# Two rates for the attention filler, E2's pieces split early, and priority for the factor of each norm

## The chip, the cores and the metric

The kernel runs on one core of one Trainium2 chip. The metric is the device time of one execution in microseconds (us); the time of a kernel is the median over several runs. All products are fp32: every operand is split into a high and a low part of the type fp32r, and three matmuls (high by high, high by low, low by high) make one product. Most of the work of ACT and DVE is to make these parts: ACT casts the high part, DVE subtracts it from the source to get the low part.

## The reference, cut to what matters

```python
D_MODEL, SEQ, DEPTH = 1024, 512, 2      # one layer of each kind
MLA_HEADS, NOPE_DIM, ROPE_DIM, V_DIM = 8, 128, 64, 128
B_HEADS, B_HEAD_DIM = 16, 64
...
# layer 0: x = x + post_norm(mla_mixer(pre_norm(x)));   x = x + post_norm(swiglu(pre_norm(x)))
# between: k_band, v_band = shared_kv(x)
# layer 1: x = x + post_norm(chunked_mixer(pre_norm(x), k_band, v_band));  x = x + post_norm(swiglu(pre_norm(x)))
def rms_norm(x, g):
    return x * lax.rsqrt(jnp.mean(x * x, axis=-1, keepdims=True) + EPS) * g
def swiglu(h, w_gate, w_up, w_down):
    return (jax.nn.silu(h @ w_gate) * (h @ w_up)) @ w_down
# a mixer: q, k, v by projections; p = softmax(q k^T + bias or mask); (p v) @ w_o
```

## The kernel before

The 512 rows of x are held transposed, features on the partitions, as eight tiles of 128x512. The stages follow one another: projections, the first attention (8 heads), its out product with `w_o`, a norm, the feed-forward part with its down product, a norm, the shared keys and values, the second attention (16 heads), its out product, a norm, the feed-forward part, and a last norm that writes the output.

A framework places the instructions on the engines by a priority that follows the order in which the code records them; each engine then runs its list in order, and waits there for whatever an instruction needs. `first(n)` records what stands inside it with a priority n earlier.

*Attention.* `attention()` runs over slots, one for each head and query tile of 128 rows. A slot makes the scores (tiles `sc`, from `qh`, `ql`, `kh`, `kl`) and their softmax: a DVE operation that adds the bias and takes the row's extreme (`mn`), then an ACT exponential. Two slots later the probabilities are transposed and split (`turn`, tiles `pth` and `ptl`), and later all of a head is multiplied with its values (`pv`). Between these steps `weave(upto)` takes matmuls from the `Filler`, a generator of units: the projections of the coming heads, then the first three of seven products of the out product. `upto` is the number of units that should be done by this slot; it grows at one rate from `first` to `units`. If head h begins and its projection is not done, `start_a(h)` forces the rest of it at once (`fill.until`).

*Out and down products.* They use seven block products in place of eight: A11, A22, A12, E1, E2, E3 and E6 are products of sums and differences of blocks. For the out product the order is A11, A22, A12, E2, E3, E1, E6. `Rows` makes the left operands, `os` tiles of 128x512 that hold two 128x256 pieces each; a product in its list `now` has each piece split (tiles `ph`, `pl`) as soon as it exists, any other has whole tiles split shortly before use (`ahead`).

```python
self.w, self.rows, self.banks = w, Rows(KT, w.order, lambda n: U(name="os"),
                                        (Seven.A22, Seven.A12, Seven.A11)), {}
```

`seven()` runs the remaining four products in groups of weight tiles; `post.during(j, group)` is called after each group, `post.product(j, ...)` after each product.

*The norm behind a product.* `After.put` (L1146 to L1150) copies a first product's bank into a tile `y`, adds a second bank to it (DVE), and takes its square with a sum per row (ACT, tiles `sq` and `ss`). `rstd` and `power` make the factor: two small DVE operations (`ssv`), then a power on POOL (`r`, L1182). `scale` (L1190) multiplies the `y` tiles with it on ACT. `turn` (L1209) transposes them on TensorE (`yt`), adds the result to `x` (L1212), and splits the new x for the feed-forward part (`xh`, `xl`, L150 and L151). The rows are done in two halves of 256. The second half's transposes stand within the first matmuls of the feed-forward part: `half(0)` gives 18 of its products, each three matmuls of 128x256 on `xh` and `xl`, then `post.turn(1)` follows. Before, `fetch` loads the eight tiles of x (SP's queue) before the remaining four products begin.

Weights are loaded by DMA into `raw` tiles (five buffers) and split into `whi` and `wlo` (three buffers each). `U` tiles, 40 buffers, serve for x, pieces, `y` and much else.

Of the kernel before, what the change touches and what calls it, by code (L numbers as in the profile page):

```python
# [21 lines left out]
H_A, NOPE, ROPE, VD = 8, 128, 64, 128  # L22
QL, KVL = 384, 256
H_B, HD = 16, 64
# [44 lines left out]
def trunk(ctx: ExitStack, tc: tile.TileContext, a, out):  # L69
# [57 lines left out]
    G_APRE, G_APOST, G_FPRE, G_FPOST = (0, 1), (2, 3), (4, 5), (6, 7)  # L127
# [25 lines left out]
    class Pair:  # L153
# [4 lines left out]
        def __init__(self, src):  # L158
            self.src, self.raw = src, {}
# [29 lines left out]
    class Seven:  # L189
# [23 lines left out]
        def fetch(self, to, i, q):  # L213
            n, src, tag = self.width(i), self.src[q, i], self.homes[to][i]
            if tag in ("u", "h"):
                parts = []
                for c in range(0, n, S):
                    t = U(name="wd") if tag == "u" else wide[0].tile([P, S], F32, tag="h", name=name_("wd"), bufs=2 * NF - 4)
                    nc.sync.dma_start(t, src[:, c:c + S])
                    parts.append(t)  # L220
            else:
                t = (wp if tag == "raw" else wide[0]).tile([P, 1024], F32, tag=tag, name=name_("raw"),
                                                           bufs=5 if tag == "raw" else 2)
                nc.sync.dma_start(t[:, :n], src[:, :n])
                parts = [t[:, :n]]
            self.at[to, i] = parts
# [129 lines left out]
    def halves_of(make):  # L356

        return lambda: [(make(), make()) for _ in range(2)]
# [29 lines left out]
    def cut(t, c):  # L388
        return t[0][:, c], t[1][:, c]
# [125 lines left out]
            q_ = slice(qt * P, (qt + 1) * P)  # L515
            split(self.pt[0][:, :qt + 1, q_], self.pt[1][:, :qt + 1, q_], tv)

    def attention(n_heads, start, fill, first, units, after):


        slots = n_heads * NQT
        heads, done, late = {}, [0], []
        rate = (units - first) / slots

        def weave(upto):
            n = 0
            while (n < 4 if fill.scored else done[0] < upto) and fill.step():
                done[0] += 1
                n += 1

        for i in range(slots + 3):
            h, qt = divmod(i, NQT)
            if h < n_heads:
                if qt == 0:
                    heads[h] = start(h)
                    if h == 0:
                        weave(first)
                heads[h].scores(qt)
                fill.scored = i == slots - 1
            weave(first + rate * (i + 0.5))  # L540
            if late and not after:
                late.pop()()
            if i >= 6 and i % NQT == 2:
                t = heads.pop((i - 6) // NQT)
                late.append(t.pv(*t.pt))
                fill.weighed = not heads
            if 2 <= i < slots + 2:
                t, qt = divmod(i - 2, NQT)
                heads[t].turn(qt)
            if late and i % NQT == 3:  # L550
                late.pop()()
            weave(first + rate * (i + 1))
        if late:
            late.pop()()

# [132 lines left out]
    class Out:  # L688
# [2 lines left out]

        def __init__(self, w):
            self.w, self.rows, self.banks = w, Rows(KT, w.order, lambda n: U(name="os"),
                                                    (Seven.A22, Seven.A12, Seven.A11)), {}

        def first(self):
            late = []
# [74 lines left out]
    x = []  # L772
# [19 lines left out]
    xs, sx = [], Sum()  # L792
    b1 = [bank() for _ in range(3)]
    for k in range(KT):
        h, l = U(F32R, "xh"), U(F32R, "xl")
# [66 lines left out]
    for j in range(2):  # L862
        V.tensor_tensor(ckv[j], ckv[j], rkv, op=OP.mult)
        h, l = U(F32R, "ckh"), U(F32R, "ckl")
# [9 lines left out]
    for j in range(3):  # L874
        h, l = U(F32R, "cqh"), U(F32R, "cql")
# [134 lines left out]
        return Head(qk, lambda n: mask[:, S - n:], lambda qt: nsq[:, qt:qt + 1], pv, sums)  # L1010

    fill = Filler(fill_a())
    attention(H_A, start_a, fill, 13, 8 + 5 * 7 + 6 + 6, False)
    fill.drain()
    st.close()

# [1 line left out]
    def ffn(i, x_src, oo):  # L1018
        hp = tc.tile_pool(name=f"ffn{i}", bufs=1, reuse_waits="tile")
        st = ExitStack()  # L1020
        hp = st.enter_context(hp)

        wide[0] = hp

        def H(dt=F32, name="h"):
            return hp.tile([P, S], dt, tag="h", name=name_(name), bufs=2 * NF - 4)

        feed.room["h"] = halves_of(lambda: H(F32R, "wh"))
        post = After(G_APOST[i], None, H)
        post.x = fetch(x_src)  # L1030
        sx = post.split = Split(post.x, G_FPRE[i], H)
        oo.rest(post)
        x, xs = post.x, sx.xs
        banks = [bank() for _ in range(4)]
        ws = []

        def half(h):
            for c in range(4):
                if not h:
                    ws.append(feed.next(1024))  # L1040
                for k in (2 * c, 2 * c + 1):
                    for j in range(4):
                        mm3(banks[j][:, HALF[h]], ws[c]((k % 2) * S + j * P, P), cut(xs[k], HALF[h]),
                            k == 0, k == KT - 1)
                        yield

        rest = half(0)
        some(rest, 18)
        post.turn(1)
        run(rest)  # L1050
        sx.squares(0)
        run(half(1))
        sx.squares(1)
        for k in range(KT):
            nc.sync.dma_start(a["mid"][:, k], x[k])
        tb = []
        more = blocks_of(x, G_FPRE[i], H, tb)
# [12 lines left out]
        hid = Rows(NF, range(7), lambda n: (U if n >= NF - 2 else H)(name="hd"))  # L1070


        for f in range(N_WHOLE):
            if f < 3:
                b = banks[2 * f:2 * f + 2]
                if f == 2:
                    run(rest)
            else:
                b = [bank(), bank()]
                run(proj(2, KT, 4, xs, b))  # L1080
            t = U(name="gt")
            V.tensor_tensor(t, b[0], rb, op=OP.mult)
            nc.scalar.activation(t, t, AF.Silu)
            h = hid.make()
            V.scalar_tensor_tensor(h, t, -1.0, b[1], op0=OP.mult, op1=OP.mult)
            hid.add(h)
            if f == 1:
                next(more)
        products(xs, tb, rb, hid)
        post = (AfterLast if i else AfterDown)(G_FPOST[i], eps, U)  # L1090
        seven(hid, down_weights(None), 0, ((0,), (1,), (2,), (3,), (4, 5)), post,
              {j: [bank(tag) for _ in range(2)] for j, tag in ((Seven.A11, "mm"), (Seven.A22, "t"), (Seven.A12, "mm"),
                                                               (Seven.E1, "s"))})
        st.close()
        return post
# [29 lines left out]
    class After:  # L1125
# [30 lines left out]
        def product(self, j, banks):  # L1156
            for o, h in {Seven.A11: ((0, 0),), Seven.A12: ((0, 0),), Seven.A22: ((1, 0),), Seven.E1: ((1, 1),),
                         Seven.E2: ((0, 1),), Seven.E3: ((1, 0), (1, 1)), Seven.E6: ((0, 1),)}[j]:
                if j == Seven.E3 and h and self.y[o][2]:
                    self.later = [lambda: self.put(1, 1, banks)] + self.later  # L1160
                else:
                    self.put(o, h, banks)
                if j == Seven.E3 and not h:
                    self.rstd(0)
                if j == Seven.E6:
                    self.rstd(1)

        def rstd(self, h):

# [15 lines left out]
                self.later.append(do) if i < 2 else do()  # L1185

        def scale(self, i, r):
            for o in (1, 0) if i >= 2 else (0, 1):
                t = self.y[o][i]
                nc.scalar.activation(t, t, AF.Copy, scale=r)  # L1190

        def during(self, j, i):

            if j == Seven.E1 and i == 0:
                while self.later:
                    self.later.pop(0)()
            if j == Seven.E6 and i == 0:
                self.turn(0)
# [131 lines left out]
    post = ffn(0, a["x"], oo)  # L1330
# [11 lines left out]
    x, sx = post.x, post.split  # L1342
    xs = sx.xs
# [117 lines left out]
    fill = Filler(fill_b())  # L1461
# [12 lines left out]
    for tt in range(NQT):  # L1474
        v_split(b[tt], 1, tt)

    attention(H_B, start_b, fill, 12, 7 * 16 + 6, True)
    fill.drain()
    st.close()

# [90 lines left out]
```

## Time and profile before

| | before |
|---|---|
| median of 3 runs | 1171.3 us (1171.22 to 1173.81) |
| profiled execution | 1172.23 us |
| its span | 1170.5 us, 1.73 us less |
| granted TensorE clock, mean | 0.986 |
| busy: PE, DVE, ACT, POOL | 1124.7, 968.2, 710.6, 80.6 us |
| DMA | 153.96 MB, mean 132 GB/s |

The times of single instructions come from the profiled execution. "Busy" is the time in which an engine ran at least one instruction; PE is TensorE's matmuls and PEld its weight loads, DVE is VectorE, ACT ScalarE, POOL GpSimd, SP SyncE. A row of the timeline begins with its start and its duration, then engine, line of the kernel, operation, output <- input; in brackets stand the idle time of the engine just before it and the instruction whose end ended that idle time. The granted clock is the share of full speed that TensorE was given.

### The profile page before, as it was taken

How to read it: one execution, taken by the hardware profiler on the slowest of the kernel's cores; microseconds unless marked ns; L12 is line 12 of the kernel's file. 1: busy time of each engine (PE TensorE's matmuls, PEld its weight loads, DVE VectorE, ACT ScalarE, POOL GpSimd, SP SyncE). 2: the span in 40 equal slices, each digit the busy share in tenths (PEclk: the TensorE clock that was granted, in tenths of full speed). 3: DMA queues.
4: the chain of work that ended last, by engine and by line, in shares of the span. 5: the costliest groups of instructions: out<-in, count | busy, mean ns of one | idle time of the engine just before them, and what ended most of it. 6: DMA issues, size and time to landing. Idle time of an engine off the chain costs nothing. (4 is left out here: it accounts for less than half of the span.)

```text
span 1170.5 us, 18810 instructions
## 1 busy us (share of the span) xinstructions
PE 1124.7 (96%) x6781; PEld 984.1 (84%) x6781; DVE 968.2 (83%) x1729; ACT 710.6 (61%) x1397; POOL 80.6 (7%) x106
## 2 busy tenths in 40 slices
PE   9999999999999999999999999888999999999996
PEld 6787878889999997787887777667999999987785
DVE  7787678799989888979768876877889899888967
ACT  6475658755555556678436665767755555556574
POOL 1200020100000002400000000010000000002400
PEclk9999999899999999999999999999999999999999
DMA  7332273413332448941446656583422323349901
GB/s 228 117 100 78 78 168 120 163 61 103 103 114 91 135 163 226 204 128 60 160 144 160 152 145 161 151 211 97 138 89 92 109 90 98 128 163 251 201 8 72
DMA packets 65868, 153.96 MB, mean 132 GB/s; under 512 B 8752, under 2 KB 10544, under 8 KB 65776
## 3 DMA queue, kind: packets, MB, share of 16 engines
q1 hardware_dynamic: 56992, 137.00, 37.5%
q0 software_dynamic: 8640, 15.73, 8.0%
q8 instruction: 53, 0.87, 0.3%
q14 instruction: 39, 0.32, 0.1%
q10 hardware_dynamic: 144, 0.04, 0.0%
HBM read 121.61 MB, written 8.59 MB: 111 GB/s over the span
## 5 line engine op out<-in xcount | busy, mean ns | idle before, releaser
L146 ACT CAST whi<-raw 128x1024 fp32r<-128x1024 f32 (+3 forms) x230 | 231.5, 1007 | 231.9 <-PE al L1307 78.4
L147 DVE TENSOR_TENSOR wlo<-raw,whi 128x1024 fp32r<-128x1024 f32 (+3 forms) x230 | 268.3, 1167 | 69.5 <-ACT whi L146 68.6
L661 PE MATMUL b<-whi,ph 128*128 128x512 f32 x388 | 154.3, 399 | 10.0 <-ACT ph L146 10.0
L661 PE MATMUL b<-wlo,ph 128*128 128x512 f32 x388 | 152.9, 395 | 0.6 <-DVE wlo L147 0.5
L661 PE MATMUL b<-whi,pl 128*128 128x512 f32 x388 | 152.1, 397 | 1.3 <-DVE pl L147 0.9
L1307 PE MATMUL al<-th,whi 128*128 128x256 f32 x432 | 124.2, 288 | 0.1
L1307 PE MATMUL al<-tl,whi 128*128 128x256 f32 x432 | 122.2, 283 | 0.0
L1307 PE MATMUL al<-th,wlo 128*128 128x256 f32 x432 | 122.2, 283 | 0.0
L361 PE MATMUL b<-xh,whi 128*128 128x512 f32 (+1 forms) x304 | 115.2, 382 | 1.0 <-ACT xh L150 1.0
L363 PE MATMUL b<-xh,wlo 128*128 128x512 f32 (+1 forms) x304 | 113.2, 372 | 0.0
L362 PE MATMUL b<-xl,whi 128*128 128x512 f32 (+1 forms) x304 | 113.0, 372 | 0.0
L661 PEld LDWEIGHTS b<-whi,ph 128*128 128x128 f32 x388 | 73.6, 190 | 28.2 <-ACT ph L146 13.5
L661 PEld LDWEIGHTS b<-whi,pl 128*128 128x128 f32 x388 | 73.3, 189 | 20.2 <-DVE pl L147 5.3
L661 PEld LDWEIGHTS b<-wlo,ph 128*128 128x128 f32 x388 | 73.4, 189 | 17.1 <-DVE wlo L147 3.1
L176 DVE TENSOR_TENSOR raw<-raw,raw 128x1024 f32<-128x1024 f32 x72 | 86.5, 1218 | 0.6 <-DMA raw<-in_w_pair 0.5
L1307 PEld LDWEIGHTS al<-th,whi 128*128 128x128 f32 x432 | 82.7, 191 | 2.1 <-DVE ut L1319 0.3
L146 ACT CAST whi<-wd 128x512 fp32r<-128x512 f32 x110 | 63.8, 619 | 32.1 <-PE b L661 27.1
L1307 PEld LDWEIGHTS al<-th,wlo 128*128 128x128 f32 x432 | 82.8, 192 | 0.0
L1307 PEld LDWEIGHTS al<-tl,whi 128*128 128x128 f32 x432 | 82.8, 192 | 0.0
L147 DVE TENSOR_TENSOR wlo<-wd,whi 128x512 fp32r<-128x512 f32 x110 | 72.1, 686 | 12.8 <-ACT whi L146 12.3
L501 ACT ACTIVATE p<-p,mn 128x128 f32<-128x128 f32 (+1 forms) x96 | 53.9, 562 | 33.6 <-DVE mn L499 32.9
L361 PEld LDWEIGHTS b<-xh,whi 128*128 128x128 f32 x304 | 57.7, 191 | 9.3 <-ACT xh L150 2.2
(286 smaller groups left out, 2873.9 us busy)
## 6 DMA issues: line engine op xcount, KB each, us to landing
raw<-in_w_pair SPq DMA_DIRECT2D x72, 512.0 KB, 3.6
wd<-in_w_down SPq DMA_DIRECT2D x54, 256.0 KB, 5.8
raw<-in_w_gu SPq DMA_DIRECT2D x16, 512.0 KB, 3.4
raw<-in_w_down SPq DMA_DIRECT2D x16, 512.0 KB, 4.3
raw<-in_w_qkb SPq DMA_DIRECT2D x16, 512.0 KB, 3.4
wd<-raw POOLq DMA_DIRECT2D x30, 256.0 KB, 5.5
wd<-in_w_down POOLq DMA_DIRECT2D x22, 256.0 KB, 5.1
x<-in_x SPq DMA_DIRECT2D x16, 256.0 KB, 6.4
```

The lines of the kernel that those rows point to most:

```text
L146: return (nc.scalar.copy(dst_hi, src), V.tensor_tensor(dst_lo, src, dst_hi.bitcast(F32), op=OP.subtract))
L147: V.tensor_tensor(dst_lo, src, dst_hi.bitcast(F32), op=OP.subtract))
L176: V.tensor_tensor(t, x, y, op=OP.add)
L361: nc.tensor.matmul(o, l[0], r[0], start=start, stop=False)
L362: nc.tensor.matmul(o, l[0], r[1], start=False, stop=False)
L363: nc.tensor.matmul(o, l[1], r[0], start=False, stop=stop)
L501: nc.scalar.activation(p[:, :n], p[:, :n], AF.Exp, bias=mn[:, :1], scale=-1.0, accum_out=self.sums[:, qt:qt + 1])
L661: nc.tensor.matmul(o, l[c], r[d], start=j < 4 and k == 0 and n == 0, stop=k == pairs - 1 and n == 2, skip_group_check=True)
L1307: nc.tensor.matmul(o, l[c], r[d], start=first_ and n == 0, stop=k == K2 - 1 and n == 2, skip_group_check=True)
```

## The change

1. `attention` gets `main`, a number of units and a slot: up to that slot the filler goes at one rate to that number, then at a second rate to `units`. In the first attention it goes from 13 to 49 units by slot 25, then to 57 at slot 32 (before: to 55, at one rate); in the second from 12 to 112 by slot 54, then to 120 at slot 64 (before: to 118).
2. `Out.rows` has E2 in `now` too.
3. x is loaded after the first group of E2 and not before the four remaining products.
4. In `product`, `put` and `rstd` after E6, and after the first half of E3, get a priority of 120.
5. `scale` takes the two tiles of the second half in the order 0, 1.

```diff
-    def attention(n_heads, start, fill, first, units, after):
+    def attention(n_heads, start, fill, first, main, units, after):
         slots = n_heads * NQT
-        rate = (units - first) / slots
+        knee = main[1]
+
+        def upto(x):
+            return first + min(x, knee) * (main[0] - first) / knee + max(0, x - knee) * (units - main[0]) / (slots - knee)
...
-            weave(first + rate * (i + 0.5))
+            weave(upto(i + 0.5))
...
-            weave(first + rate * (i + 1))
+            weave(upto(i + 1))
...
-                                                    (Seven.A22, Seven.A12, Seven.A11)), {}
+                                                    (Seven.A22, Seven.A12, Seven.A11, Seven.E2)), {}
...
-    attention(H_A, start_a, fill, 13, 8 + 5 * 7 + 6 + 6, False)
+    attention(H_A, start_a, fill, 13, (8 + 5 * 7 + 6, 25), 8 + 5 * 7 + 6 + 8, False)
...
-        post.x = fetch(x_src)
-        sx = post.split = Split(post.x, G_FPRE[i], H)
+        post.source, post.own = x_src, lambda x: Split(x, G_FPRE[i], H)
         oo.rest(post)
...
-                    self.put(o, h, banks)
-                if j == Seven.E3 and not h:
-                    self.rstd(0)
-                if j == Seven.E6:
-                    self.rstd(1)
+                    with first(120 if j == Seven.E6 or j == Seven.E3 and not h else 0):
+                        self.put(o, h, banks)
+                        if j == Seven.E3 and not h:
+                            self.rstd(0)
+                        if j == Seven.E6:
+                            self.rstd(1)
...
-            for o in (1, 0) if i >= 2 else (0, 1):
+            for o in range(2):
...
         def during(self, j, i):
+            if j == Seven.E2 and i == 0:
+                self.x = fetch(self.source)
+                self.split = self.own(self.x)
...
-    attention(H_B, start_b, fill, 12, 7 * 16 + 6, True)
+    attention(H_B, start_b, fill, 12, (7 * 16, 54), 7 * 16 + 8, True)
```

What this does to the order of the instructions is shown at three places. Names in the rows carry a number for the buffer's use; the lines are those of each kernel.

First, ACT in the first attention ahead of the scores of head 4, before (`pth` is the split of probabilities, `rh` a rotated query part, `whi` a weight's high part, `qh` and `kh` head 4's query and key):

```order
L146 CAST pth_1176<-pt_1310 128x4x128
L146 CAST rh_1206<-ra_1201 128x512
L146 CAST whi_1567<-raw_1252 128x1024
L146 CAST qh_1261<-b_1230 128x512
L146 CAST kh_1263<-b_1267 128x512
L146 CAST qh_1336<-b_1287 128x512
L146 CAST kh_1338<-b_1342 128x512
```

And after:

```order
L146 CAST pth_1222<-pt_1314 128x4x128
L146 CAST qh_1265<-b_1192 128x512
L146 CAST kh_1267<-b_1271 128x512
L146 CAST qh_1362<-b_1297 128x512
L501 ACTIVATE p_1287,sums_1280<-p_1287,mn_1288 128x128
L501 ACTIVATE p_1307,sums_1280<-p_1307,mn_1308 128x256
L1005 COPY of_1354<-b_1340 128x512
L146 CAST pth_1356<-pt_1358 128x128
L501 ACTIVATE p_1327,sums_1280<-p_1327,mn_1328 128x384
L146 CAST whi_1573<-raw_1243 128x1024
```

The weight's cast moved from ahead of `qh` and `kh` to behind the first scores' exponentials.

On TensorE at the same place, before (`b` is a bank, `ckh` and `ckl` the parts of the key latent, `va` the values):

```order
L361 MATMUL b_1342<-ckh_452,whi_1254 128x512
L362 MATMUL b_1342<-ckl_453,whi_1254 128x512
L363 MATMUL b_1342<-ckh_452,wlo_1255 128x512
L985 MATMUL sc_1277<-kh_1263,qh_1261 128x128
L985 MATMUL sc_1300<-kh_1263,qh_1261 128x256
L361 MATMUL b_1346<-pth_1176,va_533 128x512
```

And after:

```order
L513 MATMUL pt_1314<-ident,p_1237 128x128 x4
L361 MATMUL b_1340<-pth_1222,va_533 128x512
L362 MATMUL b_1340<-ptl_1223,va_533 128x512
L363 MATMUL b_1340<-pth_1222,va_533 128x512
L361 MATMUL b_1340<-pth_1222,va_534 128x384
...
L361 MATMUL b_1340<-pth_1222,va_536 128x128
L362 MATMUL b_1340<-ptl_1223,va_536 128x128
L363 MATMUL b_1340<-pth_1222,va_536 128x128
L989 MATMUL sc_1281<-kh_1267,qh_1265 128x128
L989 MATMUL sc_1301<-kh_1267,qh_1265 128x256
```

Where a key projection stood just ahead of the first score, the twelve matmuls of another head's `pv` now stand.

Second, ACT from the end of the second attention into its out product, before (`ph` are pieces: from `of` for A12 and E6, from `os` for the others; `y_8677` to `y_8683` the first copies of the norm, `ph_8691` E2's first tile):

```order
L1146 COPY y_8677<-b_8339 128x512
L1146 COPY y_8679<-b_8340 128x512
L146 CAST whi_8636<-raw_7890 128x1024
L146 CAST ph_8197<-of_8501 128x256
L146 CAST ph_8193<-os_8188 128x256
L146 CAST whi_8703<-raw_8038 128x1024
L1146 COPY y_8681<-b_8518 128x512
L1146 COPY y_8683<-b_8519 128x512
L1150 ACTIVATE sq_8686,ss_1758_8656<-y_8677 128x512
L1150 ACTIVATE sq_8689,ss_1758_8656<-y_8679 128x512
L146 CAST ph_8691<-os_7239 128x512
```

And after (`ph_8206` and `ph_8214` are the last pieces of A22 and E2, `ph_8691` is now E3's first tile):

```order
L1150 COPY y_8677<-b_8359 128x512
L1150 COPY y_8679<-b_8360 128x512
L146 CAST ph_8691<-os_7263 128x512
L146 CAST whi_8652<-raw_7886 128x1024
L146 CAST ph_8210<-of_8494 128x256
L146 CAST ph_8214<-os_8199 128x256
L146 CAST ph_8206<-os_8201 128x256
L1150 COPY y_8681<-b_8532 128x512
L1150 COPY y_8683<-b_8533 128x512
L146 CAST whi_8695<-raw_8008 128x1024
L1154 ACTIVATE sq_8686,ss_1762_8672<-y_8677 128x512
L1154 ACTIVATE sq_8689,ss_1762_8672<-y_8679 128x512
```

E2's pieces moved from behind the copies and squares to ahead of them.

Third, ACT in the norm behind the second out product, before (`xh` is the split of the first half of the new x, `wh` of the next weight; `y_8747` and `y_8801` are the two tiles of one query tile of the second half):

```order
L150 ACTIVATE xh_8936<-x_8671,gains 128x256
L150 ACTIVATE xh_8941<-x_8673,gains 128x256
L1150 ACTIVATE sq_8968,ss_1758_8656<-y_8747 128x512
L1150 ACTIVATE sq_8971,ss_1758_8656<-y_8749 128x512
L146 CAST wh_9011<-raw_8867 128x512
L1190 ACTIVATE y_8801<-y_8801,r_8975 128x512
L1190 ACTIVATE y_8747<-y_8747,r_8975 128x512
L1190 ACTIVATE y_8803<-y_8803,r_8975 128x512
L1190 ACTIVATE y_8749<-y_8749,r_8975 128x512
```

And after:

```order
L150 ACTIVATE xh_8944<-x_8729,gains 128x256
L146 CAST wh_8957<-raw_8849 128x512
L150 ACTIVATE xh_8949<-x_8731,gains 128x256
L1154 ACTIVATE sq_8976,ss_1762_8672<-y_8755 128x512
L1154 ACTIVATE sq_8979,ss_1762_8672<-y_8757 128x512
L146 CAST wh_9019<-raw_8875 128x512
L146 CAST wh_9021<-raw_8875 128x512
L1196 ACTIVATE y_8755<-y_8755,r_8983 128x512
L1196 ACTIVATE y_8809<-y_8809,r_8983 128x512
L1196 ACTIVATE y_8757<-y_8757,r_8983 128x512
L1196 ACTIVATE y_8811<-y_8811,r_8983 128x512
```

The squares still stand behind the last `xh`; the tile that was scaled second is scaled first.

On DVE at the same place, before (`xl`, `wlo` and `wh` are low parts, L1148 the adds into `y`, `ssv` the second half's factor before the power):

```order
L147 TENSOR_TENSOR wh_8950<-raw_8841,wh_8949 128x512
L151 SCALAR_TENSOR_TENSOR xl_8937<-x_8671,gains,xh_8936 128x256
L1148 TENSOR_TENSOR y_8747<-y_8747,be_8675 128x512
L151 SCALAR_TENSOR_TENSOR xl_8942<-x_8673,gains,xh_8941 128x256
L1148 TENSOR_TENSOR y_8749<-y_8749,be_8676 128x512
L147 TENSOR_TENSOR wlo_9046<-raw_8945,whi_9045 128x1024
L1180 SCALAR_TENSOR_TENSOR ssv_8658<-ss_1758_8656,ssv_8658 128x2
L147 TENSOR_TENSOR wlo_9126<-raw_9009,whi_9125 128x1024
L147 TENSOR_TENSOR wh_9012<-raw_8867,wh_9011 128x512
```

And after, where the two adds stand 18 and 15 rows ahead of the `ssv`:

```order
L1152 TENSOR_TENSOR y_8755<-y_8755,be_8675 128x512
...
L1152 TENSOR_TENSOR y_8757<-y_8757,be_8676 128x512
...
L151 SCALAR_TENSOR_TENSOR xl_8945<-x_8729,gains,xh_8944 128x256
L147 TENSOR_TENSOR wh_8958<-raw_8849,wh_8957 128x512
L151 SCALAR_TENSOR_TENSOR xl_8950<-x_8731,gains,xh_8949 128x256
L147 TENSOR_TENSOR wlo_9054<-raw_8953,whi_9053 128x1024
L1186 SCALAR_TENSOR_TENSOR ssv_8674<-ss_1762_8672,ssv_8674 128x2
L147 TENSOR_TENSOR wh_9020<-raw_8875,wh_9019 128x512
L147 TENSOR_TENSOR wlo_9134<-raw_9017,whi_9133 128x1024
L147 TENSOR_TENSOR wh_9022<-raw_8875,wh_9021 128x512
```

The adds moved up; the `ssv` kept its place behind the splits of x and of one weight, and one more weight split stands behind it.

More of the change, by code (lines that the diff above doesn't have):

```diff
@@ L1029, in ffn @@
         post = After(G_APOST[i], None, H)
-        post.x = fetch(x_src)
-        sx = post.split = Split(post.x, G_FPRE[i], H)
+        post.source, post.own = x_src, lambda x: Split(x, G_FPRE[i], H)
         oo.rest(post)
-        x, xs = post.x, sx.xs
+        x, sx = post.x, post.split
+        xs = sx.xs
         banks = [bank() for _ in range(4)]
```

## The prediction

> **What bounds the kernel now.** The page's head and its table of engines come first, then the waits of TensorE over the span (microseconds, number, longest).
>
> ```profile
> span 1170.5 us, 18810 instructions
> PE 1124.7 (96%) x6781; PEld 984.1 (84%) x6781; DVE 968.2 (83%) x1729; ACT 710.6 (61%) x1397; POOL 80.6 (7%) x106
> ```
>
> ```profile
> PE b L661 <- ACT ph L146: 10.0, 8, 3.4
> PE yt L1209 <- ACT y L1190: 5.2, 3, 2.5
> ...
> PE sc L985 <- ACT kh L146: 1.9, 1, 1.9
> ```
>
> TensorE is busy for 1124.7 of 1170.5 us, and the change takes no matmul away. So only its idle time (45.8 us) and the time at which it runs slowly can go. The change touches all three of the waits shown: the pieces `ph` of an out product (L661), the scaled `y` ahead of a norm's transposes (L1209), and one head's keys `kh` (L985).
>
> Next, windows of 3.4 or 6.8 us around the longest of them: PE's busy time and matmuls, PEld, DVE, ACT, POOL, then the granted clock, the DMA share and GB/s.
>
> ```profile
> 107.98:111.39 3.41, 1.53 (x7) 0.86 (x5) 2.73 (x4) 2.54 (x5) 0.00 (x0) 1.00 0.38 88
> 111.39:118.22 6.83, 6.44 (x23) 5.91 (x23) 3.63 (x10) 2.25 (x7) 0.00 (x0) 0.50 0.52 142
> 203.55:206.97 3.42, 1.20 (x8) 1.00 (x8) 2.15 (x4) 1.09 (x3) 2.21 (x1) 1.00 0.59 168
> 206.97:213.79 6.82, 6.12 (x29) 6.12 (x30) 3.45 (x8) 6.08 (x16) 0.00 (x0) 0.50 0.57 162
> 439.07:442.49 3.42, 1.87 (x7) 0.89 (x6) 3.07 (x6) 2.27 (x5) 0.00 (x0) 1.00 0.00 0
> 753.10:756.51 3.41, 1.85 (x12) 1.28 (x12) 2.93 (x8) 3.03 (x9) 0.00 (x0) 1.00 0.85 262
> 756.51:759.92 3.41, 2.95 (x12) 2.29 (x10) 3.41 (x10) 1.78 (x6) 1.82 (x2) 0.50 1.01 354
> 780.41:783.82 3.41, 0.96 (x4) 0.82 (x5) 2.10 (x4) 3.41 (x10) 0.00 (x0) 1.00 1.06 411
> 783.82:787.23 3.41, 3.41 (x10) 2.63 (x9) 2.73 (x5) 1.60 (x4) 0.00 (x0) 0.50 0.96 382
> 814.54:817.95 3.41, 1.21 (x8) 1.00 (x8) 2.96 (x5) 1.23 (x3) 2.10 (x1) 1.00 0.56 175
> 817.95:824.78 6.83, 5.30 (x25) 5.30 (x26) 3.08 (x8) 5.95 (x14) 0.11 (x1) 0.50 0.56 163
> ```
>
> A wait here costs more than itself. Where PE was busy for 0.96 to 1.85 us of such a window, the granted clock was 0.50 for the next one or two windows; after 1.87 us of 3.42 (at 439.07) it stayed at 1.00. Work done at half clock takes twice as long, so half the busy time of a 0.50 window is lost as well. A wait that shrinks until its window holds over 1.9 us of work should give back both.
>
> **The change part by part.** The profiled execution took 1172.23 us, 0.93 over the median of 1171.3; the sum goes against it, and 0.93 comes off at the end.
>
> *(a) The faster filler, first attention.* At the start of head 4 (columns: start, duration, instruction, idle before):
>
> ```profile
> 108.85 1.04 ACT L146 CAST whi<-raw 128x1024 fp32r<-128x1024 f32 x1 [1.23 <-PE b L362]
> 110.28 0.59 ACT L146 CAST kh<-b 128x512 fp32r<-128x512 f32 x1
> 110.92 0.50 PE L985 MATMUL sc<-kh,qh 128*128 128x128 f32 x2 [1.88 <-ACT kh L146]
> 111.81 0.80 PE L361 MATMUL b<-pth,va 128*128 128x512 f32 x1 [0.39 <-DVE ql L147]
> 160.08 0.50 PE L361 MATMUL b<-pth,va 128*128 128x512 f32 x1 [0.67 <-ACT pth L146]
> 749.29 0.50 PE L1432 MATMUL b<-ptl,vb 128*128 128x512 f32 x1 [0.33 <-DVE ptl L147]
> ```
>
> Before, `start_a` forces out the rest of head 4's projection; ACT casts a weight (1.04, itself held 1.23 for a free buffer), then `kh`, and PE waits 1.88 + 0.39 = 2.27. In the new order head 4's `qh` and `kh` are cast ahead of that weight, and twelve matmuls of another head's values stand between the projection and the scores. These need `pth` and `ptl` on their part; elsewhere such matmuls waited 0.67 and 0.33, so I leave 1.0 (ends 0 and 2.27). Gain 1.27. The window at 107.98 then holds about 1.53 + 1.27 = 2.8 us of work, and the half clock of 111.39 goes: 6.44 / 2 = 3.2. Together 4.5.
>
> *(b) E2's pieces, first out product.* The first two rows are its waits for pieces, the third a wait for a weight.
>
> ```profile
> 168.97 0.50 PE L661 MATMUL b<-whi,pl 128*128 128x512 f32 x1 [0.93 <-DVE pl L147]
> 171.36 0.50 PE L661 MATMUL b<-whi,ph 128*128 128x512 f32 x1 [0.28 <-ACT ph L146]
> 175.79 0.50 PE L661 MATMUL b<-wlo,ph 128*128 128x512 f32 x1 [0.53 <-DVE wlo L147]
> ```
>
> 0.93 + 0.28 = 1.2, and I take all of it; the ends are 0 (`wlo` late instead, as the 0.53) and 2.0.
>
> *(c) E2's pieces, second out product.*
>
> ```profile
> 780.01 1.06 ACT L1146 COPY y<-b 128x512 f32<-128x512 f32 x2
> 780.97 0.64 ACT L1150 ACTIVATE sq<-y 128x512 f32<-128x512 f32 x1
> 782.20 0.61 ACT L146 CAST ph<-os 128x512 fp32r<-128x512 f32 x1
> 782.86 0.50 PE L661 MATMUL b<-whi,ph 128*128 128x512 f32 x1 [3.35 <-ACT ph L146]
> ```
>
> At the end of this attention ACT has copies, squares and casts in a row (3.41 us busy of 3.41 in the window at 780.41), and E2's first piece stands last. In the new order E2's two splits of 128x512 are four halves of 128x256; three are made within the attention, and only the last stands here, ahead of two copies, both squares and a weight. I leave 0.3 (ends 0 and 0.53, the row at 175.79) of 3.35: 3.05 gained. The window after it loses its half clock, 3.41 / 2 = 1.7. Together 4.75. Over both products that is four instructions more on ACT and on DVE; beside attention work, with DVE busy 2.73 of 3.41 at 107.98, I cost them at nothing. If that cover fails, `pth` and `ptl` come later, which is rival 2.
>
> *(d) Priority of the factor, scaling order, x later.* The last waits of both norms:
>
> ```profile
> 204.01 0.38 PE L361 MATMUL b<-xh,wh 128*128 128x256 f32 x1 [1.64 <-ACT wh L146]
> 207.68 0.69 PE L1209 MATMUL yt<-ident,y 128*128 128x128 f32 x2 [2.46 <-ACT y L1190]
> 798.32 0.71 POOL L1182 TENSOR_TENSOR r<-ssv,mhalf 128x2 f32<-128x2 f32 x1 [24.92 <-DVE ssv L1180]
> 813.86 0.28 PE L362 MATMUL b<-xl,wh 128*128 128x256 f32 x1
> 813.98 0.28 PE L363 MATMUL b<-xh,wh 128*128 128x256 f32 x1
> 815.85 2.21 POOL L1182 TENSOR_TENSOR r<-ssv,mhalf 128x2 f32<-128x2 f32 x1 [16.81 <-DVE ssv L1180]
> 815.88 0.39 PE L361 MATMUL b<-xh,wh 128*128 128x256 f32 x1 [1.62 <-ACT wh L146]
> 819.48 0.69 PE L1209 MATMUL yt<-ident,y 128*128 128x128 f32 x2 [2.40 <-ACT y L1190]
> ```
>
> The priority moves DVE's adds into `y` some ten rows up. But the factor's chain goes through ACT's two squares, and these still stand behind all eight `xh` casts; ahead of the last `ssv` DVE has the same work as before. So the factor comes no earlier. Behind `ssv` DVE now has three splits instead of two ahead of the next norm work. POOL's power took 0.71 in the row at 798.32 and 2.21 at 815.85, where DVE has two such splits: (2.21 - 0.71) / 2 = 0.75 for each, so another one may hold it 0.75 longer. On the other side, nine more 128x256 matmuls, 0.12 apart (813.86 to 813.98), stand ahead of the transposes' end: 1.05; and the tile that the first transposes read is scaled first, worth at most one ACT operation (0.64, the square at 780.97). Net, 1.05 + 0.2 - 0.75, I take +0.5 in each norm, 1.0 in all (ends twice -0.75 and twice 1.05 + 0.64: -1.5 and +3.4), and keep both norms' half-clock windows. The x loads move past one weight load on SP's queue. From E2's first matmul (782.86) to the norm's end 33 us pass over four products, so a load issued after a half of E2 has some two and a half products for itself, a cost of nothing unless x is more than 10 us late.
>
> The Trainium skill ("GPSIMD Engine Reference", section 1, Specifications) says that GpSimd shares its SBUF interfaces with VectorE and contends with DVE instructions that have two SBUF inputs. The trace agrees (0.71 against 2.21), and the rule speaks against this part.
>
> *(e) Ends of the attentions.* The filler is used up faster, so the last slots have less of it. In the order of TensorE's instructions the second attention's last head has two filler matmuls where it had six, and the four heads before it 24, 26, 25 and 18 where they had 14, 34, 17 and 21: less at the very end, a more even share ahead of it. I take 0; the ends are -2 and +2, about the idle part of one stretch like that of 753.10 to 759.92 (rival 2) lost or saved.
>
> Sum: 4.5 + 1.2 + 4.75 + 1.0 = 11.45; 1172.23 - 11.45 = 1160.8; less 0.93 is 1160.
>
> **The rivals.**
>
> *1. The waits go, the clock does not follow.* The 0.50 windows stay, or a new one opens where the same idle time lands. Then 1.27 + 1.2 + 3.05 + 1.0 = 6.5 is gained: 1165. The 1.85 and 1.87 us that fell on either side speak for it, since the limit is sharp and the waits move against the grid of windows. Against it, 2.8 us of work is far above either. The Trainium skill ("TensorE: Matmul & The Clock Gate", section "Why this matters for your kernels") wants idle gaps of about 3 us before the clock halves; by that the 2.27 us of (a) could not have caused its half clock, and (a) would give only 1.27. The trace disagrees (clock 0.50 at 111.39), so I give this 0.19.
>
> *2. Thin cover late in the second attention eats most of it.* The price of one bad stretch is in the trace already:
>
> ```profile
> 754.76 0.33 PE L1423 MATMUL sc<-k,q 128*128 128x128 f32 x1 [1.39 <-DVE mn L499]
> 757.50 1.09 PE L513 MATMUL pt<-ident,p 128*128 128x128 f32 x4 [0.46 <-DVE of L1453]
> ```
>
> 1.39 + 0.46 idle and 2.95 / 2 lost to the half clock make 3.3 us. Three such stretches more, in the last slots where DVE (3.41 of 3.41 at 756.51) has the E2 halves on top, give 1170; two and a half to four give 1168 to 1173, no change. For it: the few matmuls of the last head, and that DVE is full. Against it: the more even share of the four heads before it. 0.12.
>
> *3. The same, deciding.* From five such stretches on (16.5 us) it is slower: 1176.5. Over 0.3% slower is 1174.8, so four and a half decide. Five or six of the last slots would have to fall dry, and the new order has few matmuls only at the last head. 0.05.
>
> *4. The factor really comes early.* If ACT finishes its `xh` casts sooner, so that both norms' waits vanish, 1.64 + 2.46 + 1.62 + 2.40 = 8.1 in place of 1.0 goes, with their half clocks (6.12 + 5.30) / 2 = 5.7: 12.8 below my sum, 1147. The squares' place speaks against it. 0.08.
>
> **How the numbers follow.** My own case has 0.56. All its good ends together (1.0 + 0.8 + 0.3 + 2.4 + 2 = 6.5) would give 1153.5; its own range is 1156 (the good ends of a, b and e) to 1164 (the bad ends of b and d). The range for 8 in 10 runs from 1153 to 1169: it takes in the good ends, rival 1 and the lower half of rival 2, and leaves out rivals 3 and 4 and the rest of rival 2, 0.19. A difference of 0.3% (3.5 us) is about what can be told from no change. Faster by more: 0.56 + 0.19 + 0.08 = 0.83. Within: rival 2, 0.12. Slower: rival 3, 0.05.
>
> **What would show it.** (a) is right if no PE wait on `kh` near 110 us is over 1 us and the clock there stays at 1.00. (b), (c): no `ph` wait over 0.6 us in either out product, and 1.00 in the windows after. (d): the norms' `yt` waits still near 2 us with 0.50 behind them, and a power of POOL of 2.2 us or more. (e): PE idle in the last six slots of the second attention no longer than before. I am wrong if a new 0.50 window shows up where filler ran out, if x lands late ahead of the first transposes, or if ACT's casts move so far that the `yt` waits go.

## The result, and the profile after

The changed kernel takes 1154.95 us (median, 1153.42 to 1157.68) against 1171.26 of the kernel before, run beside it: a ratio of 0.9861 with a 95% interval of 0.9833 to 0.9889, 16.3 us less. The prediction said 1160 and 1153 to 1169. One execution of a kernel further below (the later x alone) had a granted clock of 0.747 and took 1372.25 us; no number here uses it.

The head of the page after, and TensorE's waits over the span as they answer to those shown of before:

```profile
span 1154.5 us, 18807 instructions
PE 1113.9 (96%) x6781; PEld 979.3 (85%) x6781; DVE 968.2 (84%) x1733; ACT 710.0 (61%) x1401; POOL 87.2 (8%) x106
```

```profile
PE b L665 <- ACT ph L146: 6.3, 5, 1.7
PE yt L1218 <- ACT y L1196: 4.9, 3, 2.2
PE bc L474 <- POOL r L457: 4.5, 2, 2.3
PE b L363 <- DVE wh L147: 1.9, 2, 1.1
```

The span fell by 16.0 us, of which 10.8 are PE's busy time (the same 6781 matmuls, in part at a better clock) and 5.2 its idle time. The longest `ph` wait went from 3.4 to 1.7 (what is left lies in the down products, which the change doesn't touch), the wait on `kh` is gone, the `yt` waits are nearly what they were, and one wait is new: `bc`, the factor of the feed-forward part spread over the partitions, waits 4.5 us for POOL.

Where it went is seen when both spans are cut at the same places. The stages are: first attention and out product to the first norm transposes; that norm up to the first pair of feed-forward blocks; from there to the second attention's first score; second attention and out product; its norm; the rest. First before, then after, with the columns of the windows above:

```profile
64.65:191.90 127.25, 121.83 (x636) 100.71 (x636) 96.14 (x214) 82.06 (x191) 7.97 (x9) 0.97 0.40 112
191.90:251.15 59.25, 55.15 (x342) 50.04 (x341) 50.82 (x107) 39.69 (x80) 4.73 (x2) 0.94 0.32 107
251.15:614.08 362.93, 358.08 (x2291) 323.44 (x2290) 308.70 (x470) 209.86 (x370) 22.51 (x28) 1.00 0.46 135
614.08:803.63 189.55, 178.01 (x906) 141.81 (x904) 147.99 (x340) 126.98 (x313) 9.72 (x22) 0.98 0.60 157
803.63:862.57 58.94, 54.84 (x341) 49.66 (x340) 50.78 (x106) 39.35 (x78) 4.74 (x2) 0.94 0.33 108
862.57:1170.50 307.93, 294.97 (x2007) 271.06 (x2005) 264.44 (x396) 173.81 (x303) 21.57 (x25) 0.99 0.43 122
```

```profile
64.79:183.98 119.19, 117.21 (x636) 98.74 (x636) 95.93 (x216) 82.38 (x195) 7.90 (x9) 1.00 0.43 120
183.98:242.46 58.48, 52.99 (x342) 47.37 (x340) 50.70 (x106) 38.86 (x78) 7.95 (x2) 1.00 0.32 109
242.46:605.85 363.39, 357.76 (x2291) 323.49 (x2290) 309.07 (x470) 209.64 (x370) 22.70 (x28) 1.00 0.46 135
605.85:787.11 181.26, 174.26 (x905) 142.09 (x904) 148.00 (x342) 127.28 (x315) 9.73 (x22) 0.99 0.63 164
787.11:846.75 59.64, 54.17 (x342) 48.74 (x340) 50.89 (x107) 39.30 (x80) 7.95 (x2) 0.97 0.31 107
846.75:1154.50 307.75, 294.93 (x2007) 271.04 (x2005) 264.49 (x396) 173.81 (x303) 21.57 (x25) 0.99 0.42 122
```

Both attentions with their out products gained all of it: 127.25 to 119.19 is 8.06 us, 189.55 to 181.26 is 8.29. The norms together gained 0.07 (59.25 to 58.48, and 58.94 to 59.64): PE was busy 2.2 us less in the first, at a better clock, and idle 1.4 us longer. The rest moved by less than half a microsecond.

Around the places that the prediction names, the timeline and the 3.4-us windows after read:

```profile
107.78 0.50 PE L361 MATMUL b<-pth,va 128*128 128x512 f32 x1 [0.67 <-ACT pth L146]
108.50 0.50 PE L362 MATMUL b<-ptl,va 128*128 128x512 f32 x1 [0.22 <-DVE ptl L147]
199.87 0.44 PE L1218 MATMUL yt<-ident,y 128*128 128x128 f32 x2 [2.19 <-ACT y L1196]
226.96 0.65 PE L474 MATMUL bc<-ident,r 128*128 128x128 f32 x4 [2.14 <-POOL r L457]
773.37 0.50 PE L665 MATMUL b<-whi,ph 128*128 128x512 f32 x1 [0.44 <-ACT y L1150]
```

```profile
106.04:109.45 3.41, 2.51 (x13) 1.59 (x12) 3.31 (x9) 3.08 (x8) 0.00 (x0) 1.00 0.46 109
109.45:112.86 3.41, 3.41 (x25) 3.25 (x24) 2.03 (x6) 0.50 (x2) 0.00 (x0) 1.00 0.56 148
198.22:201.63 3.41, 1.76 (x15) 1.71 (x16) 0.28 (x1) 2.54 (x5) 0.84 (x1) 1.00 0.88 280
771.64:775.05 3.41, 2.97 (x13) 2.14 (x12) 2.94 (x5) 3.41 (x7) 0.00 (x0) 1.00 1.06 404
798.95:802.36 3.41, 1.44 (x10) 1.03 (x9) 2.38 (x4) 0.45 (x1) 2.81 (x1) 1.00 0.83 291
802.36:805.77 3.41, 3.08 (x15) 3.08 (x16) 0.01 (x1) 2.73 (x6) 0.00 (x0) 0.50 0.82 263
```

At head 4 PE waits 0.89 us and its window holds 2.51 us of work, with the next at full clock; E2's first matmul in the second out product waits 0.44, for ACT's copy into `y` and no longer for a piece, again with a window well filled. Half-clock windows inside the program fell from eight (27.3 us) to two (6.8 us).

### The profile page after: what moved, and what is told of

It is laid out like the page before. It is cut to its first block, busy times and chain, and to the rows that moved or that the text cites. A ratio compares the mean times of both kernels' runs of the same rounds, so it can differ in the third digit from the quotient of the medians.

```text
span 1154.5 us, 18807 instructions
## 1 busy us (share of the span) xinstructions
PE 1113.9 (96%) x6781; PEld 979.3 (85%) x6781; DVE 968.2 (84%) x1733; ACT 710.0 (61%) x1401; POOL 87.2 (8%) x106
## 5 line engine op out<-in xcount | busy, mean ns | idle before, releaser
L363 PEld LDWEIGHTS b<-xh,wlo 128*128 128x128 f32 x304 | 57.5, 189 | 8.9
```

Of the source, the lines that this page charges most:

```text
L363: nc.tensor.matmul(o, l[1], r[0], start=False, stop=stop)
```

## The experiments

Theory A was the prediction's: each part removes its own wait. All ratios below are against the kernel before, run beside each kernel on the same chip.

**Rates alone, E2's pieces alone, both, and the norm parts alone.** The edits, in this order (the third is the first two together):

```diff
# rates: upto() with its two rates, and
+    attention(H_A, start_a, fill, 13, (8 + 5 * 7 + 6, 25), 8 + 5 * 7 + 6 + 8, False)
...
+    attention(H_B, start_b, fill, 12, (7 * 16, 54), 7 * 16 + 8, True)
# E2's pieces
-                                                    (Seven.A22, Seven.A12, Seven.A11)), {}
+                                                    (Seven.A22, Seven.A12, Seven.A11, Seven.E2)), {}
# norm parts: the fetch in during(E2, 0), and
+                    with first(120 if j == Seven.E6 or j == Seven.E3 and not h else 0):
...
+            for o in range(2):
```

> The kernel before with the two rates of the filler alone. Theory A (the parts work by themselves, as the prediction has it): the wait on kh near 110 us and its half clock go, some 4.5 to 6 us, 1165 to 1167; the waits on ph in both out products stay (0.93 + 0.28 and about 3.3). Theory B (the rates carry the change, the pieces of E2 are only what fits in afterwards): 10 us or more, below 1161.

> The kernel before with E2 among the products whose pieces are split at once, alone. Theory A: the waits of 0.93 + 0.28 and 3.35 on E2's pieces go, with the half clock behind the second, some 6 us: 1165; the wait on kh near 110 us stays at about 1.9. Theory B: no gain, 1170 to 1172, since ACT and DVE have no room for the pieces while the filler is late.

> Rates and pieces of E2 together, without the priority, the scaling order and the later x. Theory A: all of the gain of the attentions and out products, 1155, since the changed kernel's gain lies there and its norms took as long as before; the spread of x's factor over the partitions (bc) doesn't wait on POOL, so it may be 2 us below the changed kernel. Theory C (the norm parts gained several us of their own): 1159 or more.

> The kernel before with the later x, the priority and the scaling order alone. Theory A: 1170 to 1172; the norms' yt waits stay over 2 us, and if the new wait of bc on POOL's factor (2.1 and 2.3 us in the changed kernel) belongs to these parts it shows here. Theory C: 1166 or less.

| kernel | median, us | ratio | 95% interval |
|---|---|---|---|
| rates | 1165.21 | 0.9953 | 0.9938 to 0.9968 |
| E2's pieces | 1167.73 | 0.9976 | 0.9959 to 0.9994 |
| rates and E2's pieces | 1157.0 | 0.9880 | 0.9861 to 0.9899 |
| norm parts | 1165.94 | 0.9962 | 0.9948 to 0.9976 |

The rates alone came to the 6 us of theory A, and theory B falls, but the 6 us are not where theory A had them. Cut at the same places as before, the first and the fourth stage (each an attention with its out product) read:

```profile
64.80:188.97 124.17, 119.16 (x637) 99.36 (x637) 96.06 (x214) 81.88 (x192) 7.93 (x9) 0.99 0.40 115
611.05:796.89 185.84, 175.86 (x905) 143.23 (x904) 148.38 (x340) 127.59 (x313) 9.74 (x22) 0.98 0.62 160
```

That is 3.1 us shorter for the first and 3.7 for the second, where theory A had 4.5 to 6 and nothing. The second of them has as much half clock as before (6.8 us), so its gain is not the clock's.

E2's pieces alone fell between their two theories. In that trace no wait for a piece is left in either out product, and the two stages are 1.5 and 3.1 us shorter; but the third and the last stage, which it leaves as they are, are 3.2 us longer together, one with a half-clock window at 494 us that the profiled execution of before doesn't have.

Rates and E2's pieces together gave 1.2% where their sum is 0.7%. The first out product with the rates alone shows one reason:

```profile
168.16 0.50 PE L664 MATMUL b<-whi,ph 128*128 128x512 f32 x1 [3.29 <-ACT ph L146]
```

Before, the same product waited 0.93 and 0.28 for pieces. By the timelines the attention's last score comes 6.3 us earlier and the norm's first transposes only 2.9: with the faster filler PE reaches E2 before ACT has cast its pieces, and half of the gain is lost again. So the two parts need each other: in this stage the rates alone gained 3.1 us, the pieces alone 1.5, and the whole change 8.1. The norm parts were the miss: theory A gave them nothing, theory C put their 5 us into the norms, and in their trace the norms' waits had stayed. What had gone was the wait on E2's pieces. One of the two new `bc` waits, 2.3 us, was there too.

**The later x alone.**

```diff
-        post.x = fetch(x_src)
-        sx = post.split = Split(post.x, G_FPRE[i], H)
+        post.source, post.own = x_src, lambda x: Split(x, G_FPRE[i], H)
...
+            if j == Seven.E2 and i == 0:
+                self.x = fetch(self.source)
+                self.split = self.own(self.x)
```

> The kernel before with the later x load alone. The three norm parts together gave 5 us although the norms' waits stayed, and the wait on E2's first piece in the second out product fell from 3.35 to 0.50 with them. Theory D: recording x later is what did that; ACT's cast of E2's first piece then stands ahead of the squares and a weight. The waits on the pieces fall to about 0.5 each here too, 1166 to 1167.5. Theory A (the later x costs and gains nothing, the priority did it): 1171, the wait of 3.3 us stays.

> The later x alone once more, for its profile: the waits on E2's first pieces at 0.5 us or less in the second out product, and no window at half clock behind them; the wait on kh near 110 us at 1.9 and the norms' yt waits at 2.4 as before.

1165.85 us, ratio 0.9952 (0.9937 to 0.9966): all that the three norm parts gave on this base. The second run, one execution of 1169.01, shows the end of the second attention on ACT, and then PE:

```profile
777.35 1.60 ACT L146 CAST ph<-os 128x512 fp32r<-128x512 f32 x3 [1.22 <-DVE os L646]
779.96 1.07 ACT L1146 COPY y<-b 128x512 f32<-128x512 f32 x2 [1.02 <-PE b L661]
...
781.87 0.65 ACT L1150 ACTIVATE sq<-y 128x512 f32<-128x512 f32 x1
```

```profile
782.03 0.73 PE L661 MATMUL b<-whi,ph 128*128 128x512 f32 x2 [0.52 <-ACT whi L146]
783.29 0.50 PE L661 MATMUL b<-wlo,ph 128*128 128x512 f32 x1 [0.53 <-DVE wlo L147]
786.34 0.50 PE L661 MATMUL b<-whi,ph 128*128 128x512 f32 x1 [0.50 <-ACT y L1146]
```

E2's casts now stand ahead of the copies and the squares, though E2 is not in the list, and the wait of 3.35 is three of 0.5. Theory D holds. Why the scheduler puts them there when x is recorded later was not tried; that x's eight tiles come from the same 40 buffers as the pieces is only a guess. The second attention with its out product took 186.08 us in that execution, against 189.55, although there is half clock from 753 us on for two windows in place of one; the half clock behind E2's first matmul is gone.

**Rates and the later x, without E2 in the list.** The two edits above together.

> The two rates and the later x, without E2 in the list, without the priority and the scaling order. Theory D: the later x and the early splitting of E2 remove the same waits, so this comes to what the rates with E2 gave, 1156 to 1159. Rival: with the rates the first out product waits 3.3 us on E2's piece for want of time, which only the early splitting helps: 1161 or more.

1159.62 us, ratio 0.9908 (0.9887 to 0.9928), between the two expectations. Next to the rates, the later x brings 0.45%, E2's pieces 0.73%, and both together (next run) 0.84%: they remove in part the same waits (0.73% and 0.84% can't be told apart by their intervals).

**Without the priority and the scaling order.**

```diff
-                    with first(120 if j == Seven.E6 or j == Seven.E3 and not h else 0):
...
-            for o in range(2):
+            for o in (1, 0) if i >= 2 else (0, 1):
```

> The changed kernel without the priority and without the new scaling order: rates, E2's pieces and the later x. If the priority and the scaling order are worth nothing by themselves: within 0.3% of the changed kernel, 1152 to 1158, without its waits of bc on POOL (2.14 and 2.33), and with the norms' yt waits of 2.4 and half clock behind them as in the kernel before. If they are worth what separates the changed kernel from rates with E2's pieces: 1157 or more.

1156.05 us, ratio 0.9869 (0.9850 to 0.9888) against 0.9861 of the whole change: the two edits are worth nothing that can be told, and the two `bc` waits come with one of them. In its trace POOL's power in the feed-forward part took 2.52 us and no `bc` wait is left; the norms' `yt` waits are 2.38 and 2.47.

```profile
223.78 2.52 POOL L457 TENSOR_TENSOR r<-v,mhalf 128x4 f32<-128x4 f32 x1 [25.51 <-DVE v L453]
```

**DVE made to wait for POOL, in the feed-forward parts.** In the changed kernel:

```diff
         r = rstd(ss, D)
+        with first(60):
+            V.tensor_copy(small("held"), r)
```

> The changed kernel with one small copy added on DVE in each feed-forward part, which reads POOL's factor r right behind the first operation after v, so that DVE stands still until POOL is done. Theory E: POOL's power takes 5.1 us there only because DVE works without a pause; with DVE waiting it takes about 1.5, and the waits of bc (2.14 and 2.33) go: 4 us less than the changed kernel, 1151. Rival: the power itself is slow, or PE then waits for DVE's late work: 1155 and a DVE wait of several us.

1153.92 us, ratio 0.9853 (0.9838 to 0.9867). With DVE held, the power is short and the waits go, as theory E has it. POOL's power and the DVE operations beside it, first in the changed kernel, then with the copy:

```profile
221.78 5.13 POOL L457 TENSOR_TENSOR r<-v,mhalf 128x4 f32<-128x4 f32 x1 [22.72 <-DVE v L453]
...
221.66 1.10 DVE L1119 SCALAR_TENSOR_TENSOR t<-t,xg 128x256 f32<-128x256 f32 x3
...
224.81 1.23 DVE L147 TENSOR_TENSOR wlo<-raw,whi 128x1024 fp32r<-128x1024 f32 x1
```

```profile
221.78 1.18 POOL L457 TENSOR_TENSOR r<-v,mhalf 128x4 f32<-128x4 f32 x1 [22.72 <-DVE v L453]
...
221.66 0.44 DVE L1121 SCALAR_TENSOR_TENSOR t<-t,xg 128x256 f32<-128x256 f32 x1
223.00 0.17 DVE L1069 COPY held<-r 128x4 f32<-128x4 f32 x1 [0.90 <-POOL r L457]
```

DVE stands still for 0.90 us and the power takes 1.18 in place of 5.13. Both `bc` waits are gone, and each of the two stretches between the norm and the first pair of blocks is 2.4 us shorter in the trace. The medians differ by 1.0 only, within both intervals; in that profiled execution 1.6 us came back as a half-clock window in the down product (at 485 us), where the changed kernel's execution had none. So the wait's size is shown, and its worth in the median is not, here.

**The same in the norms too, and the transposes in two parts.** The first run adds the copy in the norms (`if i >= 2`, behind the power), the second also records the first half's transposes of tiles 4 to 7 behind the priority part, the third those of tiles 2 to 7:

```diff
+                    if j == Seven.E6 and type(self) is After:
+                        self.turn(0, range(4, KT, 2))
...
             nc.gpsimd.tensor_tensor(r, self.v[:, q], mhalf[:, :n], op=OP.pow)
+            if i >= 2 and type(self) is After:
+                with first(60):
+                    V.tensor_copy(small("held")[:, :n], r)
...
             if j == Seven.E6 and i == 0:
-                self.turn(0)
+                self.turn(0, range(0, 4, 2))
```

> The changed kernel with the copy on DVE that reads the factor, in the feed-forward parts and in the two norms, and the transposes as they were. If the 6 us that the two-part transposes gave came from the squares' place: the norms' power falls from 2.8 to under 1.2, the yt waits from 2.2 to 1, and the time is 1151 to 1153. If they came from POOL's freed power alone: 1148.

> The run with the waiting copy, and in the two norms behind the out products the first half's transposes of tiles 4 to 7 are recorded behind the priority part, so that ACT's two squares stand ahead of half of the xh casts; a copy on DVE that reads r stands there too. Theory F: the last yt waits of 2.2 us come from the squares' place behind the casts; they go, and the half-clock windows behind them: 4 to 6 us below the run with the waiting copy alone, 1146. Rival: the xh of tiles 4 to 7 come later and PE waits for these in the next product by as much: no gain or a loss.

> The version with waiting copies and two-part transposes, but only the first pair of tiles (0 and 1) ahead of the priority part and six tiles behind it. The factor comes about 1 us earlier, for which nothing waits any more; the casts of tiles 2 to 7 come later, and PE may wait for these in the first product behind the norm. Same time as with half and half, 1146 to 1149, if the casts still keep ahead; 2 us more for each norm if they don't, 1151.

| kernel | median, us | ratio | 95% interval |
|---|---|---|---|
| copies in feed-forward parts and norms | 1147.05 | 0.9790 | 0.9773 to 0.9807 |
| and transposes in two parts, four and four | 1147.65 | 0.9794 | 0.9775 to 0.9812 |
| and transposes in two parts, two and six | 1145.99 | 0.9788 | 0.9766 to 0.9810 |

I had put the second of these down to the squares' place behind the `xh` casts (theory F). It ran first and gave the 6 us I expected, for another reason: the copies alone give the same. In the first norm, before the copy (the changed kernel) and with it:

```profile
196.24 2.81 POOL L1188 TENSOR_TENSOR r<-ssv,mhalf 128x2 f32<-128x2 f32 x1 [17.23 <-DVE ssv L1186]
...
197.81 0.69 DVE L147 TENSOR_TENSOR wh<-raw,wh 128x512 fp32r<-128x512 f32 x1
```

```profile
195.91 1.07 POOL L1190 TENSOR_TENSOR r<-ssv,mhalf 128x2 f32<-128x2 f32 x1 [17.23 <-DVE ssv L1188]
...
197.79 0.44 PE L1223 MATMUL yt<-ident,y 128*128 128x128 f32 x2 [0.46 <-ACT y L1201]
```

The power falls from 2.81 to 1.07, the `yt` wait from 2.19 to 0.46, and PE is then busy for 2.84 us of the window from 194.88 to 198.29, with full clock behind it: that profiled execution has one half-clock window inside the program, at 1027.73 us. The two-part transposes bring the power to 0.70 and the waits to about nothing, which is worth no more in the medians. By their ratios these three versions beat the changed kernel by about 0.7%; the one with the copies alone is the simplest.

## Why the prediction was right, and where it was not

The time lay in the range, 5 us below the value. The waits that the prediction names went, but their worth was spread otherwise over its steps. By these:

- *(a) Filler, first attention: right in the wait.* The wait left is 0.89 (I had left 1.0) and the half clock at head 4 is gone. With the rates alone the stage gained 3.1 where I had 4.5: by then E2's first piece made PE wait 3.29, with a half-clock window behind it. I had added (a) and (b) as if they didn't meet; next to the rates, the other parts are worth 5.0 there (124.17 to 119.19) where (b) had 1.2.
- *(b) and (c) E2's pieces: right in the waits, wrong in the cause.* No wait for a piece is left in either out product, and next to the rates the other parts gained 4.6 in the second (185.84 to 181.26) where (c) had 4.75. But I costed the later x at nothing and gave E2's list the whole, while the later x alone moves the casts ahead. The order of the instructions of each part by itself would have shown that; I had read the change as one.
- *(d) Priority: the sum was nearly right, by luck.* I took +1.0 and both norms together gave 0.07, as two errors that nearly cancel. Better than said: of the four half-clock windows of the two norms one was left in this execution. That too is partly chance: PE was busy for 1.76 us of the window behind the first norm's wait (198.22), a value at which the clock dropped in some executions and not in others. Worse: the power beside three splits took 2.81 (I had 2.96), but I followed it only to the norm, and the next power, in the feed-forward part, took 5.13 in place of 2.52 and cost 2.14 and 2.33. The rule of the Trainium skill that I set beside this, that GpSimd contends with DVE instructions with two SBUF inputs ("GPSIMD Engine Reference", section 1, Specifications), was the one to follow through: the traces agree with it beyond what I had priced (5.13 with DVE at work, 1.18 with DVE held), though one power took 1.18 beside a working DVE, as the last section shows. With DVE kept still in norms and feed-forward parts the changed kernel gained another 7.9 us, rival 4's time by another way than I gave it; how much of that the priority has a share in was not tried.
- *(e) Ends of the attentions: put at nothing, and 3.7.* The second attention with its out product gained that with the rates alone, outside the ends of -2 and +2 that I gave. 1.6 of it is idle time and 2.1 PE's busy time, with as much half clock as before. I had looked there only for what the last slots might lose. Why PE's same matmuls take less time there was not tried. Rivals 2 and 3 did not come; one half-clock window remained near the end of that attention, as before (at 744.33 for 756.51).
- *The sums.* With (a) and (b) I had 5.7 us, measured 8.06: 1.0 of the surplus is idle time (the wait of 0.53 for a weight went too, and one of 0.35) and 1.4 busy time that I can't assign. With (c) and (e) I had 4.75, measured 8.29, and (e) is the surplus. That the total came within 5 us owes something to (d), which had 0.9 too much.
- *Rival 1* (the clock wouldn't follow) was wrong for these windows. The rule of the Trainium skill of about 3 us of idle time ("TensorE: Matmul & The Clock Gate", section "Why this matters for your kernels") does not describe these runs; the next section but one gives the numbers.

## What to carry to other kernels

Build each part of a change alone and read the order that comes out before crediting one of them: here the line that looked like housekeeping moved the casts as much as the line that was meant to. Cut the trace of each part into stages too: the rates alone gave about the time that was expected, and more than half of it in a place where nothing was. A gain upstream counts only as far as the next supplier keeps up; the faster rates alone lost half of what they won in the first attention to the next wait. And where a small operation on POOL sits in a chain, look whether DVE pauses beside it: letting DVE wait for 1 us freed up to 4.

## What the runs showed of the hardware that I had not expected

**A pause of DVE lets POOL's power end, but it doesn't always need one.** The 128x4 power in the changed kernel ended at 226.91, 0.87 us after DVE's last operation (224.81 + 1.23). Before, in the first feed-forward part, it ended 0.86 after a pause of 0.20 in DVE's row began:

```profile
232.57 2.52 POOL L457 TENSOR_TENSOR r<-v,mhalf 128x4 f32<-128x4 f32 x1 [26.32 <-DVE v L453]
...
233.82 0.41 DVE L147 TENSOR_TENSOR tl<-t,th 128x256 fp32r<-128x256 f32 x1
234.44 1.22 DVE L176 TENSOR_TENSOR raw<-raw,raw 128x1024 f32<-128x1024 f32 x1 [0.20 <-DMA raw<-in_w_pair]
```

(234.23 to 235.09, with DVE at work again from 234.44.) With the copy it ended at 222.96, 0.86 after 222.10. The 128x2 power in the changed kernel's norm ended at 199.05, 0.55 after 198.50. So in these four 0.86 or 0.87 us (128x4) and 0.55 (128x2) pass from the start of DVE's pause. Other powers ended without one. With the norm parts alone the first feed-forward part's took 1.18, while DVE ran operations with two inputs back to back until 233.30:

```profile
229.04 1.18 POOL L457 TENSOR_TENSOR r<-v,mhalf 128x4 f32<-128x4 f32 x1 [23.95 <-DVE v L453]
228.94 1.09 DVE L1115 SCALAR_TENSOR_TENSOR t<-t,xg 128x256 f32<-128x256 f32 x3
229.95 1.08 DVE L147 TENSOR_TENSOR tl<-t,th 128x256 fp32r<-128x256 f32 x3
```

In the same execution's second part the same DVE operations stood beside a power of 5.13, and in the second part of the kernel before a power took 2.52 with no pause of DVE until 848.30. What lets POOL through there these runs don't show. That a pause does is shown by the copies: with them every power in these places took 0.69 to 1.19 us.

**The clock drops after a window half idle, not after one idle.** In thirteen profiled executions, on the grid of 3.41-us windows and up to 14 us before the end, every one of the 27 full-clock windows with PE busy for 1.62 us or less was followed by one at 0.50. Of 60 with 1.69 to 2.06 us, 19 were; of the more than 4100 with more, none. So there is no sharp limit between 1.85 and 1.87, as the prediction had it from two windows. The grid starts 3.9 to 7.2 us after the first instruction, differently in each execution, so a wait of 1.5 to 2.5 us falls into one window or is shared between two by chance. A removed wait of that size pays in some executions and not in others; this is a likely part of the 0.3% between runs, and why a difference between two profiled executions is not yet one between kernels.
